# Turned gated features moved through another engine's DMA queue, and split later

## The chip, the cores and the metric

One NeuronCore of a Trainium2 chip runs the whole program. The engines are TensorE (PE, matrix products), VectorE (DVE), ScalarE (ACT), GpSimd (POOL) and SyncE (SP), each with its own queue of instructions that it works through in order. A transfer (DMA) is issued by an instruction in one of these queues; the queues of SP, ACT and POOL can issue, and an issue that waits for something holds up what stands behind it in that queue. The metric is the device time of one execution in microseconds, lower is better. Before the change it is 1006.37 us, the median of three runs (1005.99 to 1008.15).

## What is computed

A decoder trunk of two layers over 256 tokens of width 1024, in float32. Each layer is:

```
h = h + 1/2 * FFN1(norm(h))          # silu(x Wg) * (x Wu), then Wd; inner width 2816
h = h + mixer(norm(h))               # 8 stick-breaking heads and 4 latent-attention heads
h = h + 1/2 * FFN2(norm(h))
h = h + sigmoid(norm(h) Wgate) * (p[layer] Wproj)
```

A final norm follows. There are four FFNs in the program (two layers, `a` before the mixer and `b` behind it), and the change lies in them alone.

## The kernel before

**Split products.** A float32 product is made of three matmuls on reduced operands: each operand is split into a high part `h` and the rest `l`, and the sum takes high by high, high by low and low by high (`mm3`, lines 254 to 259; the three matmuls are lines 256, 257, 258). So every weight passes three engines before PE: a load by SP into a `raw` buffer (7 of them), ACT makes `wh`, DVE makes `wl`. A pair `wh`, `wl` of 1024 columns is a tile of the pool `w`, of which there are 8. `Unit.load` (from line 140) does this for plain weights (load line 148, `wh` 152, `wl` 153). `Seven` (from line 174) does it for blocks that are multiplied with seven products in place of eight; there DVE first adds and subtracts raw blocks (line 188) and then ACT and DVE split the sums (lines 193, 194; loads line 185).

**An FFN.** The inner width is cut into six blocks (`NBLK`): five of 512 columns and a last one of 256. For each block `i` PE makes the gate `g` and the up-projection `u` for both token halves `t` (0 and 1), 128 tokens each. Blocks 1 and 3 (only 3 in the first FFN of the program) are made by `wide_seven`, which starts with seven products on sums of quarters of `x` (14 calls of `mm3`) and ends with two half products (`half_mm`, 16 calls). `gated` then makes `silu(g) * u` into the tile `pr` (DVE, line 540) and calls `Gates.add`.

**Turning the features (`Gates.add`).** The down-projection needs the features on the partitions, not the tokens. `add` does it in steps: DVE transposes `pr` in blocks of 32 by 32 (line 502); a transfer `m` writes `pr` to a buffer in DRAM (line 504); four transfers read it back, one per group of 32 partitions, into the tile `a`, which the profile calls `ft` (`back`, line 509); ACT and DVE split `ft` into `fh` and `fl` (`parts`, lines 516, 517); and for blocks 1, 2, 3 the second half also makes four sums of the two halves and splits them (`sums`, lines 469 to 480). The `ft` tiles come from the tag `w2`, which has two buffers, so a block's pair must be read before the next block's pair can be written. All these transfers are issued from SP, in the same queue as the loads of the weights. A block sends 2 transfers `m` and 8 transfers `ft`; there are 24 blocks in the program.

**The down phase.** After the six blocks PE multiplies with the down weights: two chunks of block 0, then seven products on block 1, the rest of block 0, seven on block 2, block 5, seven on block 3, and block 4. Behind the first seven products everything still due is emitted (`flush`). In the middle of this phase `ple_inputs` loads `p` from SP (line 1007) into a buffer that block 0's features had.

**What sets the order.** The program is written down in PE's order. `soon(us, f)` puts a step off by so many microseconds of PE work: `mm3` adds 0.68 to a running sum for 512 columns, and steps that are due are written down there. `BACK` is the delay of `back`, `PARTS` that of `parts`, both from the call of `add`. A planner then orders each engine's queue by the order in which the program was written and by when, by its own reckoning, operands and buffers are ready. So a queue is not exactly in the written order: in the profile DVE does line 471 ahead of line 517 of the same half, for example. `after` only forbids an order; the split `fh` may not come ahead of the newest `wh` written before it.

Of the kernel before, what the change touches and what calls it, by code (L numbers as in the profile page):

```python
# [32 lines left out]

BACK, PARTS = 2.5, 7.0


def turned_order(n):
# [25 lines left out]
def trunk(ctx: ExitStack, tc: tile.TileContext, xT, xr, pT, w, gains, fgain, consts, out):  # L65
    nc = tc.nc
# [47 lines left out]
    def after(later, earlier):  # L114

        tc.add_manual_dep(later.ins, earlier.ins.name, mybir.DependencyInfo(mybir.DependencyClass.NoSync, mybir.DependencyReason.DATA), reason="order")
# [119 lines left out]
    def soon(us, f):  # L236
        due.append((pe[0] + us, len(due), f))
# [23 lines left out]
    def both(x, *ix):  # L261
        return tuple(t[ix] for t in x)
# [22 lines left out]
    def wt(tag, name, n=2, width=T):  # L285

        return tp.tile([P, 768], F32, tag=tag, name=name)[:, : n * width].rearrange("p (a b) -> p a b", a=n)
# [7 lines left out]
    def in_runs(x):  # L295

        return x.rearrange("p j (a s) -> p j a s", s=32)
# [29 lines left out]
    class Norm:  # L327
# [8 lines left out]
        def add(self, t, c):  # L336

            i = self.parts[t]
            self.parts[t] += 1
            junk = flat("w3", f"junk_{self.name}_{t}{i}", BF16)[:, : c.stop - c.start]  # L340
            return nc.scalar.activation(junk, h[:, t, c], AF.Square, accum_out=self.ss[:, t, i : i + 1])
# [90 lines left out]
    class Gates:  # L432
# [63 lines left out]
        def add(self, i, t, pr, more):  # L496


            f = self.block(i)
            n = 4 if i < NBLK - 1 else 2  # L500
            name = f"{self.tag}_{i}{t}"
            nc.vector.transpose(pr, pr)
            m = mem_p.tile([P, 4, n * 32], F32, tag="turn", name=f"m_{name}")
            nc.sync.dma_start(m, pr.rearrange("p (q r) -> p q r", q=4))
            a = wt("w2", f"ft_{name}", 4, n * 32)

            def back():
                for q in range(4):
                    nc.sync.dma_start(a[32 * q : 32 * q + 32], m[:, q].rearrange("(a f) r -> f a r", a=4))

            def parts():
                self.turned[i, t] = v = a.rearrange("p a (j s) -> p j a s", j=n)

                ks = slice(2 if i in SEVEN and t else 0, n)
                fh, fl = (in_runs(q) for q in both(f, slice(None), ks, slice(t * P, (t + 1) * P)))
                after(nc.scalar.activation(fh, v[:, ks], AF.Copy), newest_wh[0])
                nc.vector.tensor_tensor(fl, v[:, ks], fh.bitcast(F32), ALU.subtract)
                if i in SEVEN and t:
                    self.sums(i)

            soon(BACK, back)
            soon(PARTS + t, parts)

    def seven_mm(banks, x_of, ops, first, last):

# [698 lines left out]
```

## Time and profile before

| | |
|---|---|
| median of three runs | 1006.37 us |
| profiled execution, whole | 1003.63 us |
| its span, first to last instruction | 1001.8 us |
| mean granted TensorE clock | 0.996 |
| PE busy | 981.6 us (98%) |
| DVE busy | 861.9 us (86%) |
| ACT busy | 635.7 us (63%) |
| POOL busy | 12.4 us (1%), 13 instructions |
| DMA moved | 210.50 MB, 210 GB/s over the span |

The profile records one execution. A busy time is the sum of an engine's instructions; instructions that issue transfers are not counted in it. A row of the timeline gives start, duration, engine, source line, operation, output and input names, and in brackets the idle time before it with what ended it; rows with `x3` at the end hold three instructions in a row. `SPq` is SP issuing transfers. A row of the waits gives who waited for whom: total time, number of times, the longest. Line numbers are those of the kernel before.

### The profile page before, as it was taken

To read this page: it belongs to the slowest core of one execution; us is meant where nothing else is said; L and a number is where in the kernel's file an instruction comes from. 1 tells how busy PE (TensorE), PEld (TensorE's weight loads), DVE (VectorE), ACT (ScalarE), POOL (GpSimd) and SP (SyncE) were. 2 spreads that over 40 slices of the span, in tenths; PEclk is the share of its full clock that TensorE was granted. 3 is DMA by queue.
4 is the path that set the end of the run, shared out by engine and by line. 5 is a ranking of instruction groups with operands and counts; after the bars stand their busy time and mean duration, and the time that the engine had idled before them with its cause. 6 is when DMAs were issued, how large, how long until landed. Compare 5 with 4: busy or idle time off the path is not lost.

```text
span 1001.8 us, 14087 instructions
## 1 busy us (share of the span) xinstructions
PE 981.6 (98%) x4888; PEld 824.2 (82%) x4888; DVE 861.9 (86%) x1218; ACT 635.7 (63%) x974; POOL 12.4 (1%) x13
## 2 busy tenths in 40 slices
PE   9998999999999999999999999999999999999996
PEld 7875888899888888887788888888998888888875
DVE  6689999967679999799998998899676799989995
ACT  6746656848566566567676556567766755756664
POOL 0000000000100000000000000002000000000000
PEclk9999999999999999999999999999999999999999
DMA  8876875675233778685737686676733357776651
GB/s 302 302 252 202 302 231 188 230 257 175 98 127 108 268 224 274 197 259 194 262 105 264 229 272 213 212 249 210 274 106 106 126 174 251 267 240 204 222 187 43
DMA packets 88055, 210.50 MB, mean 210 GB/s; under 512 B 14000, under 2 KB 35632, under 8 KB 87984
## 3 DMA queue, kind: packets, MB, share of 16 engines
q1 hardware_dynamic: 87552, 209.03, 62.1%
q8 instruction: 38, 0.62, 0.2%
q10 hardware_dynamic: 432, 0.57, 0.2%
q14 instruction: 33, 0.27, 0.1%
HBM read 196.98 MB, written 12.58 MB: 209 GB/s over the span
## 4 chain that ended last, share of the span: by engine, by line
PE 86%; DVE 5%; DMA 4%; ACT 3%; issue 1%; SPq 0%; ACTq 0%; DVEq 0%
DMA raw<-in_w 4%; PE p_b L256 3%; PE g_a L256 3%; PE p_b L257 3%; PE g_a L258 3%; PE g_a L257 3%; PE g_b L257 3%; PE g_b L258 3%; PE g_b L256 3%; PE p_b L258 3%; PE d_a L257 3%; PE d_a L258 3%; PE d_a L256 3%; PE p_a L257 3%; PE p_a L258 3%; PE p_a L256 2%
## 5 line engine op out<-in xcount | busy, mean ns | idle before, releaser
L153 DVE TENSOR_TENSOR wl<-raw,wh 128x1024 fp32r<-128x1024 f32 (+1 forms) x278 | 321.0, 1187 | 49.5 <-ACT wh L152 48.1
L152 ACT ACTIVATE wh<-raw 128x1024 fp32r<-128x1024 f32 (+1 forms) x278 | 278.5, 1031 | 103.2 <-DMA raw<-in_w 47.4
L193 ACT ACTIVATE wh<-raw 128x1024 fp32r<-128x1024 f32 x133 | 139.0, 1058 | 130.0 <-DVE raw L188 98.9
L194 DVE TENSOR_TENSOR wl<-raw,wh 128x1024 fp32r<-128x1024 f32 x133 | 159.4, 1216 | 11.1 <-ACT wh L193 10.4
L188 DVE TENSOR_TENSOR raw<-raw,raw 128x1024 f32<-128x1024 f32 x76 | 92.6, 1220 | 4.5 <-DMA raw<-in_w 2.4
L256 PE MATMUL d_a<-wh,fh_a 128*128 128x512 f32 x108 | 42.3, 391 | 0.0
L258 PE MATMUL d_b<-wh,fl_b 128*128 128x512 f32 x108 | 42.2, 391 | 0.0
L256 PE MATMUL d_b<-wh,fh_b 128*128 128x512 f32 x108 | 42.2, 391 | 0.0
L258 PE MATMUL d_a<-wh,fl_a 128*128 128x512 f32 x108 | 42.1, 390 | 0.0
L257 PE MATMUL d_b<-wl,fh_b 128*128 128x512 f32 x108 | 42.1, 389 | 0.0
L257 PE MATMUL d_a<-wl,fh_a 128*128 128x512 f32 x108 | 42.0, 389 | 0.0
L256 PE MATMUL g_a<-wh,x0h 128*128 128x512 f32 x80 | 31.1, 390 | 0.3 <-ACT x0h L305 0.3
L257 PE MATMUL g_a<-wl,x0h 128*128 128x512 f32 x80 | 31.0, 389 | 0.0
L258 PE MATMUL g_a<-wh,x0l 128*128 128x512 f32 x80 | 31.0, 389 | 0.0
L257 PE MATMUL u_a<-wl,x0h 128*128 128x512 f32 x64 | 25.2, 394 | 0.5 <-DVE wl L153 0.5
L256 PE MATMUL g_b<-wh,x_mix0h 128*128 128x512 f32 x64 | 25.1, 392 | 0.0
L256 PE MATMUL g_b<-wh,x_mix1h 128*128 128x512 f32 x64 | 25.1, 392 | 0.0
L256 PE MATMUL g_a<-wh,xe0h 128*128 128x512 f32 x64 | 25.0, 391 | 0.0
L258 PE MATMUL u_a<-wh,x0l 128*128 128x512 f32 x64 | 25.0, 390 | 0.0
L258 PE MATMUL g_a<-wh,xe0l 128*128 128x512 f32 x64 | 24.9, 390 | 0.0
L257 PE MATMUL g_a<-wl,xe0h 128*128 128x512 f32 x64 | 24.9, 389 | 0.0
L258 PE MATMUL g_b<-wh,x_mix0l 128*128 128x512 f32 x64 | 24.9, 389 | 0.0
(552 smaller groups left out, 2683.9 us busy)
## 6 DMA issues: line engine op xcount, KB each, us to landing
raw<-in_w SPq DMA_DIRECT2D x338, 512.0 KB, 5.1
m_a<-pr_a SPq DMA_DIRECT2D x20, 256.0 KB, 2.1
ft_a<-m_a SPq DMA_DIRECT2D x80, 64.0 KB, 2.7
m_b<-pr_b SPq DMA_DIRECT2D x20, 256.0 KB, 2.3
ft_b<-m_b SPq DMA_DIRECT2D x80, 64.0 KB, 2.9
raw<-in_w SPq DMA_DIRECT2D x16, 256.0 KB, 4.4
xin<-in_xT SPq DMA_DIRECT2D x4, 256.0 KB, 4.7
h<-in_xr SPq DMA_DIRECT2D x2, 512.0 KB, 8.0
```

The costliest lines, as they stand in the source:

```text
L152: nc.scalar.activation(wh[:, a], r[:, a], AF.Copy),
L153: nc.vector.tensor_tensor(wl[:, a], r[:, a], wh[:, a].bitcast(F32), ALU.subtract),
L188: nc.vector.tensor_tensor(self.raw[o], self.raw[a], self.raw[b], op)
L193: newest_wh[0] = nc.scalar.activation(wh, r, AF.Copy)
L194: nc.vector.tensor_tensor(wl, r, wh.bitcast(F32), ALU.subtract)
L256: nc.tensor.matmul(o, ah, bh, start=start, stop=False, **kw)
L257: nc.tensor.matmul(o, ah, bl, start=False, stop=False, **kw)
L258: newest_mm[0] = nc.tensor.matmul(o, al, bh, start=False, stop=stop, **kw)
```

## The change

Two things change, in `Gates.add` and its two constants. The transfer `m` and the four transfers of `back` are issued from POOL's queue instead of SP's. `PARTS` goes from 7 to 12, and the second half's `parts` comes 3.5 after the first half's instead of 1; `BACK` stays.

```diff
-BACK, PARTS = 2.5, 7.0
+BACK, PARTS = 2.5, 12.0
...
             m = mem_p.tile([P, 4, n * 32], F32, tag="turn", name=f"m_{name}")
-            nc.sync.dma_start(m, pr.rearrange("p (q r) -> p q r", q=4))
+            nc.gpsimd.dma_start(m, pr.rearrange("p (q r) -> p q r", q=4))
             a = wt("w2", f"ft_{name}", 4, n * 32)
 
             def back():
                 for q in range(4):
-                    nc.sync.dma_start(a[32 * q : 32 * q + 32], m[:, q].rearrange("(a f) r -> f a r", a=4))
+                    nc.gpsimd.dma_start(a[32 * q : 32 * q + 32], m[:, q].rearrange("(a f) r -> f a r", a=4))
...
             soon(BACK, back)
-            soon(PARTS + t, parts)
+            soon(PARTS + 3.5 * t, parts)
```

## The prediction

> **What bounds the kernel now.** I read the page's totals first, then who TensorE (PE) waits for, then stretches of time.
>
> ```profile
> span 1001.8 us, 14087 instructions
> PE 981.6 (98%) x4888; PEld 824.2 (82%) x4888; DVE 861.9 (86%) x1218; ACT 635.7 (63%) x974; POOL 12.4 (1%) x13
> ```
> ```profile
> PE p_a L257 <- DVE wl L194: 3.8, 3, 2.0
> PE e L257 <- DVE wl L153: 1.7, 1, 1.7
> PE p_a L256 <- ACT wh L193: 1.6, 2, 1.1
> PE pv L257 <- DVE wl L153: 1.4, 2, 0.8
> ```
> PE is idle for 1001.8 - 981.6 = 20.2 us in all, so a change that feeds it better has little to win, and only where it waits: 5.4 us on `p_a`, the seven-product block of the first FFN, and 1.7 + 0.8 us on `e` and `pv` in layer 0's embedding stage. The stretches (PE, PEld, DVE, ACT, POOL busy; clock; DMA share; GB/s):
>
> ```profile
> 72.30:91.75 19.45, 13.82 (x47) 8.84 (x45) 19.27 (x26) 12.31 (x16) 0.00 (x0) 0.91 0.54 182
> 340.00:380.00 40.00, 40.00 (x178) 32.89 (x177) 38.27 (x50) 22.43 (x29) 0.00 (x0) 1.00 0.74 241
> 476.00:480.30 4.30, 2.45 (x12) 1.75 (x13) 3.84 (x16) 3.09 (x11) 0.00 (x0) 1.00 0.36 122
> ```
> ```profile
> 92.11 0.40 PE L258 MATMUL p_a<-wh,x0l 128*128 128x512 f32 x1
> 95.76 0.39 PE L257 MATMUL p_a<-wl,x0h 128*128 128x512 f32 x1
> ```
> From 92.11 to 95.76 PE makes 16 steps, 0.228 us each. In 72.30 to 91.75 it does 47 matmuls in 19.45 us; at its pace they take 10.7, so 8.7 us are lost there (idle time, slow restarts and a granted clock of 0.91). DVE is full in that stretch (19.27 of 19.45). In a block such as 340 to 380 DVE is nearly full too and PE loses nothing.
>
> Why is DVE late at 72? Three engines shortly before it:
>
> ```profile
> 43.77 1.32 SPq L148 DMA_DIRECT2D raw<-in_w  x3
> 51.94 1.14 SPq L504 DMA_DIRECT2D m_a<-pr_a  x2
> 53.19 0.38 SPq L148 DMA_DIRECT2D raw<-in_w  x1
> 54.02 5.59 SPq L509 DMA_DIRECT2D ft_a<-m_a  x8
> 59.66 0.91 SPq L148 DMA_DIRECT2D raw<-in_w  x2
> 60.61 1.89 SPq L185 DMA_DIRECT2D raw<-in_w  x4
> ```
> ```profile
> 49.98 1.06 ACT L152 ACTIVATE wh<-raw 128x1024 fp32r<-128x1024 f32 x1 [0.26 <-PE u_a L258]
> 59.40 1.06 ACT L152 ACTIVATE wh<-raw 128x1024 fp32r<-128x1024 f32 x1 [8.35 <-DMA raw<-in_w]
> ```
> ```profile
> 49.26 1.43 DVE L540 SCALAR_TENSOR_TENSOR pr_a<-u_a,hr_in,s_a 128x512 f32<-128x512 f32 x2 [2.97 <-PE u_a L258]
> 60.49 1.23 DVE L153 TENSOR_TENSOR wl<-raw,wh 128x1024 fp32r<-128x1024 f32 x1 [4.60 <-ACT wh L152]
> ```
> SP stands from 45.09 to 51.94 in front of the m transfer, which needs `pr`; it then sends one load, eight ft transfers, and six loads back to back in 2.84 us, so their buffers had long been free. ACT waits 8.35 us for a load and DVE 4.60 us for ACT. This is the wait that the change can take away.
>
> **The change, part by part.**
>
> *Loads no longer stand behind m and ft.* SP loses 48 m and 192 ft issues (24 blocks of two halves):
>
> ```profile
> L504 SPq DMA_DIRECT2D m_a<-pr_a x24: 326/327/382, 37.5 to 628.4; - x24
> L509 SPq DMA_DIRECT2D ft_a<-m_a x96: 302/424/1723, 39.5 to 634.5; - x96
> SPq L504 <- DVE pr_a L502: 63.9, 21, 10.2
> ```
> That is 48 x 0.327 + 192 x 0.424 = 97 us of issue time, and the `pr` waits besides. Nearly all of it hides under PE's stock of eight split tiles (12 matmuls, 2.73 us each), so it is worth nothing where PE never waits. In the first FFN it is worth this: at 49.98 ACT waited for PE, so all eight were full; by 59.40 PE had freed (59.40 - 49.98) / 2.73 = 3 more. With loads there, three `wl` splits of 1.15 us pitch go into DVE's idle 4.60 us: 3.45 us gained (bounds 0, if other waits keep DVE idle, and 4.60).
>
> *Splits stand later.* PARTS moves the first half's from 7 to 12 us of PE work after the block, the second half's, with the sums, from 8 to 15.5. In the lossy stretch block 2's lie ahead of DVE's last seven-product split:
>
> ```profile
> 86.48 1.02 DVE L517 TENSOR_TENSOR fl_a<-ft_a,fh_a 128x512 fp32r<-128x512 f32 x2
> 87.42 0.42 DVE L469 TENSOR_TENSOR sum_a<-ft_a 128x256 f32<-128x256 f32 x1
> 87.76 0.41 DVE L471 TENSOR_TENSOR sum_a<-ft_a,ft_a 128x256 f32<-128x256 f32 x1
> 88.09 0.42 DVE L470 TENSOR_TENSOR sum_a<-sum_a,ft_a 128x256 f32<-128x256 f32 x1
> 88.43 1.22 DVE L194 TENSOR_TENSOR wl<-raw,wh 128x1024 fp32r<-128x1024 f32 x1
> ```
> The seven products are 14 x 0.68 = 9.5 us of PE work, so at 12 and 15.5 these fall behind them: 88.43 - 86.48 = 1.95 us gained. They land among the half products, where one tile lasts PE 2.73 us and costs DVE 1.15: hidden. Without that cover they cost their 1.95 back. No later use is in danger: the last block's splits are flushed 14.96 us into the down phase and used at 29.9.
>
> *POOL issues 240 transfers.* No row shows its price d. Near rows, landing first:
>
> ```profile
> m_a<-pr_a SPq DMA_DIRECT2D x20, 256.0 KB, 2.1
> ft_a<-m_a SPq DMA_DIRECT2D x80, 64.0 KB, 2.7
> ```
> ```profile
> 201.31 0.73 POOL L814 TENSOR_TENSOR rk<-r_a,c_sb 128x256 f32<-128x256 f32 x1 [200.38 <-ACT r_a L362]
> 262.16 1.30 POOL L892 TENSOR_TENSOR qr<-r,r 128x512 f32<-128x512 f32 x1 [3.50 <-DVE r L890]
> 690.17 5.70 POOL L814 TENSOR_TENSOR rk<-r_a,c_sb 128x256 f32<-128x256 f32 x1 [426.72 <-ACT r_a L362]
> ```
> Below, SP's 0.33; above, POOL's own instruction held to 5.70 us (0.73 when free). I take 1.3, POOL's longest unhindered row, as the nearest to an engine that makes descriptors in a program. m0, m1 and eight ft then stand in one queue; ft waits for m to land, and behind it stand only more ft and the next block's m (POOL's arithmetic comes in the mixer, long after). For d below 2.1 the halves land 5d + 4.8 and 9d + 4.8 us after m's issue, which is 51.94 - 49.26 = 2.7 us after the block's products. Against 12 and 15.5 that is 2.0 and 3.7 us late at d = 1.3. ACT then waits, ahead of weight splits; the 8.35 us wait above cost PE 0.5 us at once, so 3.7 us inside a stock of eight tiles cost nothing: taken as 0. Where the next block follows 10.9 us after (the last one), its second ft transfer also waits for the w2 buffer until 4.6 us instead of 2.5: off the path.
>
> The 5.70 row shows POOL held up beside DVE. By the Trainium skill (SBUF — State Buffer, "Who interferes with whom") a DVE instruction with two SBUF inputs holds up a GpSimd instruction that reads SBUF, while descriptor generation, which writes, is held by DVE's two-port modes, which tensor_tensor does not have; by that rule the sum stays, without it the slow rival below comes true.
>
> *Layer 0's second FFN, 405 to 480.* The same block, but another wait takes its place:
>
> ```profile
> 413.65 0.84 SPq L148 DMA_DIRECT2D raw<-in_w  x2
> 419.81 0.81 SPq L504 DMA_DIRECT2D m_b<-pr_b  x2
> 421.60 3.92 SPq L509 DMA_DIRECT2D ft_b<-m_b  x8
> 425.57 1.38 SPq L185 DMA_DIRECT2D raw<-in_w  x3
> 427.04 0.97 SPq L148 DMA_DIRECT2D raw<-in_w  x2
> 436.40 0.33 SPq L1007 DMA_DIRECT2D p<-in_pT  x1
> ```
> The loads of 425.57 come some 4 us earlier, but the p transfer still holds SP until PE is done with a buffer at 436.40, and the lead ends there. Of the 2.5 us of stalls I take 0.5 (bounds 0 and 2.5).
>
> *Unknown:* what a first POOL transfer costs around the span (0 to 1.83, all that lies there; 0 taken), and orders that the planner changes elsewhere (plus or minus 2.5, the size of the second stall; 0 taken).
>
> **Sum:** 3.45 + 1.95 + 0.5 = 5.9 us. The profiled execution took 1003.63 (span 1001.8), so 997.7; the median of the runs is 2.74 above it, so 1006.37 - 5.9 = **1000.5 us**.
>
> **Rivals.**
> - *Nothing moves.* DVE is the bound at 60 to 92 and block 1's splits and sums, now later, go ahead of the seven products' and eat the lead. For it: DVE full. Against: they lay behind 60.49 before as well. 1006.4. The Trainium skill (DMA: Bandwidth & Descriptors, "Issuing engines are not separate DMA queues") speaks for it: issuing from several engines saves only the issue time. The row of 51.94 shows that here a wait is saved as well.
> - *Only the splits' place counts,* the planner leaving the loads where they were: -1.95, 1004.4.
> - *Both stalls go:* -8.7 - 2.5 = -11.2, 995.2.
> - *POOL is too slow.* The second half is 9d - 8.0 us late; above d = 1.8 that exceeds the 8.35 us which the stock covered. At d = 2.0 it is 10.0, 1.65 beyond; in the 11 stages of seven products (7 wide, 4 down), where DVE has no slack, that is +18 and the gain is gone: 1024. For it: the 5.70 row, DVE 86% busy. Against: 1.30 when free.
> - *The planner's new order opens a stall* like the one at `e`, and the first is kept: +2.5, 1009.
>
> **How the numbers follow.** Forecast 0.47 (its own range 998.5 to 1002.5), nothing 0.10, splits only 0.12, both stalls 0.10, slow POOL 0.14, new stall 0.07. No change can be told from below 0.2%, 2.0 us; the splits-only case lies on that bound and is halved. Faster 0.63, within 0.16, slower 0.21. The range 995 to 1010 leaves out slow POOL and part of the full cure.
>
> **What would show it.** Right: loads on SP between 45 and 52, no ACT wait of 8 us and no DVE wait of 4.6 us before 60, the 47 matmuls in about 14 us, POOL issues near 1.3 us. Wrong: ACT waiting many us for ft in block after block with PE idle behind it (slow POOL); the p_a waits as large as before with DVE full (nothing moves).

## The result, and the profile after

The changed kernel takes **1055.4 us** (median of 4 runs, 1051.7 to 1059.8) against 1006.2: ratio 1.0486, 95% interval 1.0440 to 1.0532. It is 49 us slower; the forecast was 1000.5, and the range ended at 1010.

The page's totals after the change:

```profile
span 1051.9 us, 14119 instructions
PE 996.9 (95%) x4888; PEld 827.2 (79%) x4888; DVE 861.5 (82%) x1218; ACT 632.0 (60%) x974; POOL 139.2 (13%) x253
```

The span grew by 50.1 us. PE does the same 4888 matmuls; its idle time rose from 20.2 to 1051.9 - 996.9 = 55.0 us, and 15.3 us more are counted as busy, 13.9 of them in matmuls that start within 5 us of a stop. ACT and DVE do the same work as before. So PE is fed late. Who waits for whom (total us, times, longest):

```profile
ACT fh_b L516 <- DMA ft_b<-m_b: 54.8, 14, 9.8
ACT fh_a L516 <- DMA ft_a<-m_a: 51.8, 15, 10.6
...
DVE fl_b L517 <- ACT fh_b L516: 39.0, 12, 7.3
DVE fl_a L517 <- ACT fh_a L516: 36.5, 10, 8.1
...
PE p_b L257 <- DVE wl L194: 8.8, 11, 2.5
PE p_a L257 <- DVE wl L194: 6.1, 7, 1.9
PE xt_b L371 <- DVE h L397: 5.3, 4, 2.2
PE p_b L256 <- DVE ch_b L587: 5.0, 2, 2.5
PE p_a L256 <- ACT xsh_a L562: 4.8, 1, 4.8
```

Before, the two ACT rows were 3.1 and 3.2 us. Now ACT stands 106.6 us in front of `ft`, DVE stands 75.5 us behind ACT, and PE mostly names `wl`: it waits for split weights, not for the features themselves. POOL is not slow. Its issues (duration min/median/max in ns), and the time from issue to landing in the page's list of transfers (KB each, us to landing):

```profile
L509 POOL DMA_DIRECT2D ft_a<-m_a x96: 548/551/574, 42.7 to 665.0; - x96
L504 POOL DMA_DIRECT2D m_a<-pr_a x24: 557/561/700, 39.4 to 657.7; - x24
```
```profile
m_a<-pr_a POOLq DMA_DIRECT2D x20, 256.0 KB, 2.8
ft_a<-m_a POOLq DMA_DIRECT2D x80, 64.0 KB, 5.7
```

An issue costs 0.55 us, but an `ft` transfer now takes 5.7 us to land, where it took 2.7 from SP.

**The first FFN**, where the prediction expected its gain: SP, POOL, ACT, DVE and PE in the same timeline.

```profile
44.24 1.46 SPq L148 DMA_DIRECT2D raw<-in_w  x2
46.51 8.87 SPq L185 DMA_DIRECT2D raw<-in_w  x4
...
43.80 3.25 POOL L509 DMA_DIRECT2D ft_a<-m_a  x6
...
52.17 0.63 ACT L516 ACTIVATE fh_a<-ft_a 128x512 fp32r<-128x512 f32 x1 [5.82 <-DMA ft_a<-m_a]
...
52.84 0.69 DVE L517 TENSOR_TENSOR fl_a<-ft_a,fh_a 128x512 fp32r<-128x512 f32 x1 [4.09 <-ACT fh_a L516]
...
79.52 0.79 PE L256 MATMUL p_a<-wh,xsh_a 128*128 128x512 f32 x1 [4.82 <-ACT xsh_a L562]
```

The loads do move ahead: SP, which stood from 45.09 to 51.94 in front of `m`, now sends five loads between 44.24 and 48.78, and stands only then, in front of a `raw` buffer (the row of 8.87 us holds that wait, 49.11 to 55.05). But ACT's 8.35 us wait for a load has become one of 5.82 us for `ft`, and DVE's 4.60 one of 4.09.

**A down phase**, where the loss is. The `ft` of block 5, both halves, are issued from 147.91 on (a row of eight issues); ahead of them a wait of block 3:

```profile
119.32 0.63 ACT L516 ACTIVATE fh_a<-ft_a 128x512 fp32r<-128x512 f32 x1 [6.42 <-DMA ft_a<-m_a]
...
147.91 4.40 POOL L509 DMA_DIRECT2D ft_a<-m_a  x8 [4.18 <-DMA m_a<-pr_a]
...
153.56 0.42 ACT L516 ACTIVATE fh_a<-ft_a 128x256 fp32r<-128x256 f32 x1 [5.61 <-DMA ft_a<-m_a]
153.88 2.94 ACT L193 ACTIVATE wh<-raw 128x1024 fp32r<-128x1024 f32 x3
...
154.01 0.42 DVE L517 TENSOR_TENSOR fl_a<-ft_a,fh_a 128x256 fp32r<-128x256 f32 x1 [2.77 <-ACT fh_a L516]
154.35 3.49 DVE L194 TENSOR_TENSOR wl<-raw,wh 128x1024 fp32r<-128x1024 f32 x3
...
155.63 0.50 PE L257 MATMUL p_a<-wl,fh_a 128*128 128x512 f32 x1 [1.11 <-DVE wl L194]
```

ACT waits 5.61 us for a split of 0.42; the three `wh` behind it are done back to back in 2.94 us as soon as it moves, so their operands had been ready. DVE loses 2.77 us, then does three `wl` in a row, and PE waits for the first. The 6.42 us wait at 119, in the plain blocks, cost PE nothing on the spot. It took from the stock. Counting the weight splits `wl` that DVE has begun when PE starts its matmul of a given number:

```
matmul of mm3 number      400    500    600
before                     49     60     70
changed                    47     57     66
changed with PARTS 36      51     59     69
```

The changed kernel is two splits short when the down phase begins (60 begun against 62, matmul 523) and four short at 600, of a pool of eight tiles. From 140 to 200 in the trace before, DVE is busy for 56.68 of 60 us, so there it cannot catch up. (The third row is an experiment below.)

To place the loss I compared the start of each matmul with that of the same number in the trace before. The lag (us), and where it grows:

```
stage                                    added
first FFN (up to 100, end of the wide 7)  -0.8   (lag +2.8 at 80, -0.8 at 100)
4 down phases (140-200, 429-480, 625-690, 905-960)   7.4 + 6.2 + 11.2 + 11.6 = 36.4
wide sevens of the later FFNs (360-380, 565-580, 850-890)  5.5 + 2.8 + 5.4 = 13.7
everything else                          -0.2
at 960 us of the trace before            +49.1
```

Nothing is lost in plain blocks. All of it is lost in the stages with seven products and at the end of the down phases, where PE waits 9.5 us in all for `h` (`xt_a` and `xt_b`; no such wait before).

### The profile page after: what moved, and what is told of

Same layout as the page of the kernel before. It is cut to its first block, busy times and chain, and to the rows that moved or that the text cites. A ratio compares the mean times of both kernels' runs of the same rounds, so it can differ in the third digit from the quotient of the medians.

```text
span 1051.9 us, 14119 instructions
## 1 busy us (share of the span) xinstructions
PE 996.9 (95%) x4888; PEld 827.2 (79%) x4888; DVE 861.5 (82%) x1218; ACT 632.0 (60%) x974; POOL 139.2 (13%) x253
## 4 chain that ended last, share of the span: by engine, by line
PE 37%; issue 24%; DVE 17%; DMA 15%; ACT 4%; POOL 2%; SPq 0%; POOLq 0%; ACTq 0%; DVEq 0%
DVE wl L194 5%; DMA raw<-in_w 4%; DMA ft_b<-m_b 4%; DVE wl L153 4%; DVE raw L188 3%; DMA ft_a<-m_a 3%; ACT wh L152 2%; DMA m_b<-pr_b 2%; PE e L258 1%; PE e L256 1%; PE e L257 1%; DMA m_a<-pr_a 1%; PE g_a L258 1%; PE g_a L256 1%; PE g_b L257 1%
## 5 line engine op out<-in xcount | busy, mean ns | idle before, releaser
L152 ACT ACTIVATE wh<-raw 128x1024 fp32r<-128x1024 f32 (+1 forms) x278 | 278.8, 1030 | 101.5 <-DMA raw<-in_w 35.3
L193 ACT ACTIVATE wh<-raw 128x1024 fp32r<-128x1024 f32 x133 | 136.8, 1053 | 115.5 <-DVE raw L188 112.1
L509 POOL DMA_DIRECT2D ft_a<-m_a x96 | 52.4, 553 | 29.9 <-DMA m_a<-pr_a 21.2
L509 POOL DMA_DIRECT2D ft_b<-m_b x96 | 52.4, 553 | 29.3 <-DMA m_b<-pr_b 17.0
L504 POOL DMA_DIRECT2D m_a<-pr_a x24 | 13.6, 566 | 275.2 <-DVE pr_a L502 274.4
L504 POOL DMA_DIRECT2D m_b<-pr_b x24 | 13.5, 563 | 258.2 <-DVE pr_b L502 257.5
L516 ACT ACTIVATE fh_b<-ft_b 128x512 fp32r<-128x512 f32 (+1 forms) x24 | 12.9, 536 | 54.8 <-DMA ft_b<-m_b 54.8
L517 DVE TENSOR_TENSOR fl_b<-ft_b,fh_b 128x512 fp32r<-128x512 f32 (+1 forms) x24 | 13.9, 578 | 39.0 <-ACT fh_b L516 39.0
L516 ACT ACTIVATE fh_a<-ft_a 128x512 fp32r<-128x512 f32 (+1 forms) x24 | 12.9, 537 | 51.8 <-DMA ft_a<-m_a 51.8
L517 DVE TENSOR_TENSOR fl_a<-ft_a,fh_a 128x512 fp32r<-128x512 f32 (+1 forms) x24 | 13.8, 576 | 36.5 <-ACT fh_a L516 36.5
```

The source lines that it names most:

```text
L152: nc.scalar.activation(wh[:, a], r[:, a], AF.Copy),
L193: newest_wh[0] = nc.scalar.activation(wh, r, AF.Copy)
L504: nc.gpsimd.dma_start(m, pr.rearrange("p (q r) -> p q r", q=4))
L509: nc.gpsimd.dma_start(a[32 * q : 32 * q + 32], m[:, q].rearrange("(a f) r -> f a r", a=4))
```

## The experiments

The ratios are to the kernel before, run on the same chip, with 95% intervals.

### Which part does it: the queue or the later splits

Queue alone:

```diff
-            nc.sync.dma_start(m, ...)        +            nc.gpsimd.dma_start(m, ...)
-                    nc.sync.dma_start(a[...  +                    nc.gpsimd.dma_start(a[...
 BACK, PARTS = 2.5, 7.0      # and PARTS + t, as before
```

> Only the queue is changed: m and ft from POOL, splits where they were (7 and 8 us). Theory A (ScalarE parks at the split fh until the turned features land, which through POOL's queue is some 13 us after m against 8 on SyncE, with weight splits behind it): the earlier splits meet the same late landing, so ScalarE waits for ft as long as in the changed kernel (106 us) or longer, and the time is 1050 or more. Theory B (the later splits themselves do the harm, by falling into stages where VectorE has no slack): the waits on PE go and the time is 1000 to 1010.

Measured 1057.1, ratio 1.0511 (1.0490 to 1.0532); ACT waits 104.9 us for `ft`. In ACT's queue each `fh` stands behind the same number of weight splits as in the changed kernel, or one more or less, although PARTS is 7 here.

Later splits alone, all transfers on SP:

```diff
-BACK, PARTS = 2.5, 7.0
+BACK, PARTS = 2.5, 12.0
-            soon(PARTS + t, parts)
+            soon(PARTS + 3.5 * t, parts)
```

> Only the splits are moved: 12 and 15.5 us, all transfers on SyncE as before. Theory A: ft lands 8 us after m, long before 12, ScalarE waits for ft under 10 us in all, and the time is within 5 us of before (1001 to 1011). Theory B: most of the loss is here, 1035 to 1055, with TensorE waiting for wl in the seven-product stages of the down phases.

Measured 1008.3, ratio 1.0016 (1.0006 to 1.0026). The first FFN gains 1.5 us (1.95 forecast), and 1.4 at 180 to 200, 2.2 at 440 to 480 and 0.8 at 560 to 580 are lost. So the queue costs the 49 us, and the later splits are worth about nothing at this size.

### Which of the transfers

Only `m` on POOL (`ft` on SP, PARTS 7 and t), then only `ft` on POOL (`m` on SP), then only `m` on POOL with the read-back and the splits somewhat later (BACK 4.5, PARTS 8.5, t):

> Half of the queue change, splits at 7 and 8 us: m goes from POOL, the four ft stay on SyncE. SyncE no longer stands in front of m for pr, and ft keeps its place in line among the loads. Theory A: ft lands 2.7 us after its issue as before, the stall of the first FFN at 72 to 92 us shrinks by 3 to 6 us, and the time is 1000 to 1004. If POOL's queue itself is what costs (a late m): ft is late by the 0.7 us that m lands later, SyncE waits in front of ft instead of in front of m, and the time is 1006 to 1015.

> The other half of the queue change alone, splits at 7 and 8 us: m stays on SyncE, the four ft go from POOL. Sharing theory: it is ft's place that costs. ft takes 5 us or more where loads run beside it, ScalarE waits for it more than 60 us, and the time is 1030 to 1055. If moving m is what costs, it is 1000 to 1010.

> The kernel with m on POOL and ft on SyncE, but ft written 2 us later (BACK 4.5) and the splits 1.5 later (8.5 and 9.5), so that loads may go ahead of an ft that still waits for m; SyncE stood 106 us in front of ft with BACK at 2.5. If that wait costs anything: below 998.4, 993 to 997. If it is hidden under the stock of split tiles: 997 to 1000, no change. If ft now lands too late for its split: 1002 or more, with ScalarE waiting for ft.

Measured: `m` alone **998.4**, ratio 0.9924 (0.9908 to 0.9941), below the 1000 to 1004 expected; `ft` alone 1056.0, 1.0496 (1.0469 to 1.0522), just above its 1030 to 1055; `m` with BACK 4.5 997.8, 0.9917 (0.9902 to 0.9932), not to be told from `m` alone. The whole loss is in `ft`'s queue; `m`'s move is a gain that the change threw away. The transfers of the kernel with only `m` moved, and its first FFN:

```profile
ft_a<-m_a SPq DMA_DIRECT2D x80, 64.0 KB, 2.0
```
```profile
43.92 1.38 SPq L509 DMA_DIRECT2D ft_a<-m_a  x3
45.40 2.27 SPq L148 DMA_DIRECT2D raw<-in_w  x5
57.98 3.65 SPq L509 DMA_DIRECT2D ft_a<-m_a  x8
...
75.90 0.50 PE L257 MATMUL p_a<-wl,xsh_a 128*128 128x512 f32 x1 [2.18 <-DVE wl L194]
```

This is the test of the prediction's main term. SP sends five loads at 45.40, in the stretch in which it stood before, and ACT's 8.35 us wait is gone (waits of at most 1.79 us are left). DVE does use the early loads: at matmul 240 it has begun 32 weight splits against 29 before. But then it waits, in its own order, for a feature split that in ACT's queue stands behind work on PE's results:

```profile
62.02 0.69 DVE L517 TENSOR_TENSOR fl_a<-ft_a,fh_a 128x512 fp32r<-128x512 f32 x1 [2.70 <-ACT fh_a L516]
```

Before, DVE began the same instruction at 61.63, and at matmul 280 both have begun 33. PE's waits on `p_a` for split weights are 4.7 us against 5.6, and at 100 us this kernel is 0.2 us behind the one before. **With the splits early, the freed loads are worth nothing there.** The gain of this kernel is elsewhere: 3.1 us at 460 to 480 (the stalls at `e` and `pv`), 1.7 at 680 to 700, 1.3 at 940 to 980.

### Does that gain come from the load of p

In the trace before SP waits 18.5 us in all in front of the two loads of `p` (line 1007), with `m` on POOL 0.6. So `p` alone on POOL, `m` and `ft` on SP:

```diff
-        nc.sync.dma_start(pr, pT[L])
+        nc.gpsimd.dma_start(pr, pT[L])
```

> The kernel before with one edit: the load of p (line 1007, two of them in the run) is issued from GpSimd. In the trace before, SP stands 8.3 us in front of the first one (428.1 to 436.4) with the weight loads behind it. Theory (the 3.1 us that the kernel with only m on GpSimd gains at 460 to 480 come from SP no longer standing in front of p): 3 us here at the same place and as much at the second layer's end, 1000 to 1003 us, with m and ft on SP as before. Rival (that gain comes from m's waits leaving SP): within 1 us of the kernel before, 1005 to 1007.

Measured 1009.3, ratio 1.0030 (1.0015 to 1.0045): 3.0 us slower, which neither expectation had, and both stalls are there:

```profile
479.69 0.50 PE L257 MATMUL pv<-wl,xpsbk 128*128 128x512 f32 x1 [1.33 <-DVE wl L153]
483.46 0.51 PE L257 MATMUL e<-wl,x_b0h 128*128 128x512 f32 x1 [1.67 <-DVE wl L153]
```

The theory falls: taking that wait out of SP's queue does not bring the gain. The same 3.07 us at 460 to 480 also appear in four kernels further down that leave `p` on SP (half loads on SP, late order on SP, and the last two); what removes the stalls there is not settled.

### Why ft lands late

First rival: POOL's way of making transfers is slow. So `m` and `ft` from ACT's queue, the rest as in the changed kernel:

```diff
-            nc.gpsimd.dma_start(m, ...)      +            nc.scalar.dma_start(m, ...)
-                    nc.gpsimd.dma_start(a... +                    nc.scalar.dma_start(a...
```

> As the changed kernel, but m and ft are issued from ScalarE's hardware queue, so they have a queue of their own without POOL's program making the descriptors. If the late landing comes from sharing the DMA engines with weight loads in another queue, ft takes 5 to 7 us to land here too. If it comes from the software path, 2.5 to 3.5 us as on SyncE. The time is not decided by this alone, since ScalarE now waits for pr and m in its own queue: 1010 to 1060.

Measured 1082.8, ratio 1.0760 (1.0736 to 1.0785). The time, above the 1010 to 1060 expected, says little itself, since ACT now also issues 240 transfers between its splits. The landing was expected at 5 to 7 us or at 2.5 to 3.5:

```profile
ft_a<-m_a ACTq DMA_DIRECT2D x80, 64.0 KB, 4.6
ft_b<-m_b ACTq DMA_DIRECT2D x80, 64.0 KB, 4.5
```

That lies between the two ranges and decides nothing. So I sorted the `ft` transfers of each trace by the number of weight loads in flight (issued and not yet landed) when the `ft` was issued (median landing in us, count in brackets; the second row is an experiment below, `m` on POOL with PARTS 36):

```
loads in flight               none         one          two        three or more
before, ft on SP            1.93 (37)   2.95 (151)   3.87 (4)        -
ft on SP, PARTS 36          1.94 (109)  2.87 (41)    4.53 (32)   5.08 (10)
changed, ft on POOL         2.19 (27)   3.46 (27)    5.04 (57)   7.22 (81)
ft on ACT                   1.96 (35)   3.57 (81)    5.65 (54)   6.54 (22)
```

Without a load in flight, `ft` lands in about 2 us from any queue; POOL's way costs 0.2. With loads in flight it lands late from every queue, and POOL is no slower than ACT up to two of them. So POOL's way is not the cause. Two things are. One is the moment of the issue: SP, which stood in front of `m` and `ft`, sent 188 of its 192 `ft` transfers with at most one load in flight; POOL sends 138 of 192 with two or more. The other is the queue: with as many loads in flight, `ft` takes some 0.5 to 2 us longer from a queue beside the loads' own. The traces show part of how. With one load in flight, a further load that SP issues within 2 us of the `ft` goes with a later landing from POOL (4.18 us against 2.79 without one) and from ACT (4.71 against 3.51), but not from SP (2.31 against 3.31). What I infer: in SP's queue that load stands behind the `ft`, from another queue it shares the DMA engines with it. How much each is worth can be estimated: SP's medians (the two and three columns from the second row), weighed by POOL's counts, give 4.2 us; POOL's own give 5.3, SP's before 2.8. So some 1.4 of the 2.5 us are the moment and 1.1 the queue.

If the loads are the cause, fewer bytes must shrink the loss. So the loads of plain weight tiles at half their bytes, in the changed kernel and, as control, in the kernel before; the second half of each such tile is left out of the computation, the first is split twice in its place:

```diff
-            newest_load[0] = nc.sync.dma_start(r, w[self.u, :, a : a + n])
+            newest_load[0] = nc.sync.dma_start(r[:, : n // 2], w[self.u, :, a : a + n // 2])
...
+                r2 = r[:, : n // 2].unsqueeze(1).to_broadcast([P, 2, n // 2])
```

> As the changed kernel, but each plain weight load moves half its bytes and ScalarE and VectorE read that half twice, so their work and PE's is the same; the second half of each such tile of weights is left out of the computation. Sharing theory (ft through another queue is slow because the weight loads take the DMA engines beside it): ft lands in 3 to 4.5 us in the median in place of 5.5, ScalarE waits for ft under 60 us, and the time falls to 1010 to 1035. If POOL's own path is slow: ft still takes 5.5 us, the waits stay near 100 us and the time at 1045 or more.

> The kernel before (all of it on SP) with the loads of the plain weight tiles cut to half their bytes: each half that is loaded is read twice by the splits, and the second half of these tiles is left out of the computation. It is the control for the changed kernel with half loads, 1012.9 us. Theory (a transfer in a second queue shares the engines with the loads, so the loss grows with the loads beside it): this kernel gains little from half loads, some 990 to 1000 us, and the changed kernel with half loads then stands 13 to 23 us above it, against 49 with whole loads. Rival (half the loads make every version faster by the same 40 us, and the loss does not hang on the loads): some 964 us, and the distance stays near 49.

Measured: changed with half loads 1012.9, ratio 1.0077 (1.0058 to 1.0097); before with half loads 986.5, 0.9806 (0.9791 to 0.9821). Their distance is 26.3 us, against 49 with whole loads. So the loss hangs on the loads, about half of it on half the plain bytes (the seven-product loads stayed whole); the 13 to 23 us of the expectation were too low, because the kernel before gained more from half loads (986.5) than the 990 to 1000 expected. The landing and ACT's waits in the changed one (its lines behind 153 count one higher):

```profile
ft_a<-m_a POOLq DMA_DIRECT2D x80, 64.0 KB, 3.6
...
ACT fh_a L517 <- DMA ft_a<-m_a: 36.8, 14, 5.7
ACT fh_b L517 <- DMA ft_b<-m_b: 27.6, 14, 5.1
```

3.6 us in place of 5.7, and 64.4 us of waits in place of 106.6, where under 60 was expected.

### Who pays: the place of the splits in ACT's queue

The changed kernel with PARTS 16 in place of 12:

> As the changed kernel (m and ft from POOL), with the splits later still: 16 and 19.5 us in place of 12 and 15.5. ft lands 10.6 and 13.0 us after m in the mean, at most 16.9, and m goes some 2.7 us after the block's products. Theory A (ScalarE parks at fh until ft lands): fh now stands behind more weight splits, the waits of ScalarE for ft fall from 106 us to under 50, and the time falls to 1010 to 1035. If where the split is written does not decide its place in ScalarE's queue (the planner puts it where it reckons that ft has landed): the waits stay near 100 us and the time stays at 1050 or more.

Measured 1055.0, ratio 1.0488 (1.0469 to 1.0506), and ACT still waits 99.0 us for `ft`. ACT's order of instructions is the same as with PARTS 12, each `fh` behind the same number of weight splits: the planner puts the split where by its reckoning `ft` is there, and 7, 12 or 16 does not bind. That was no test of a later place. With 36 and with 44, the rule that `fh` may not precede the newest `wh` written before it does bind; the `fh` of blocks 0 to 3 then stand behind 3 to 8 weight splits more with 36 and behind 5 to 12 more with 44, those of blocks 4 and 5 behind 0 to 5 more:

```diff
-BACK, PARTS = 2.5, 12.0
+BACK, PARTS = 2.5, 36.0        # second run: 44.0
```

> The changed kernel with PARTS 36 in place of 12: the splits fh then stand behind 3 to 5 more weight splits in ACT's queue in the down products (PARTS 16 had left ACT's order as it was). Nothing else is different: queues and loads are those of the changed kernel. Theory (PE pays because ACT, in order, stands in front of the late ft with weight splits behind it): ACT's waits for ft fall from 106 us to below 30, and the time to 1005 to 1025 us. Rival (the late ft itself, or the sharing of the engines with the loads, is what PE pays): ACT's waits fall as well, but the time stays at 1045 to 1056.

> As the last one with PARTS 44, 7 or more weight splits later than in the changed kernel. Theory: ACT's waits for ft are next to nothing, and if the splits are not yet so late that the products wait for them the time is the same as or a little below that with PARTS 36, 1000 to 1020 us; if they are, PE's waits name fh or fl and the time goes up again. Rival (sharing of the engines is itself the price): 1045 to 1056.

Measured **1010.5** (ratio 1.0040, 1.0025 to 1.0055) and 1010.2 (1.0037, 1.0020 to 1.0053). With 36:

```profile
ACT fh_a L516 <- DMA ft_a<-m_a: 13.8, 5, 5.3
ACT fh_b L516 <- DMA ft_b<-m_b: 13.0, 4, 6.6
...
ft_a<-m_a POOLq DMA_DIRECT2D x80, 64.0 KB, 5.5
ft_b<-m_b POOLq DMA_DIRECT2D x80, 64.0 KB, 4.6
```

`ft` still lands late (the halves 10.2 and 13.7 us after `m`'s issue in the mean, 10.6 and 13.0 in the changed kernel) and the queues are those of the changed kernel, but ACT's waits fall from 106.6 to 26.8 us, DVE's waits for `fh` behind them from 75.5 to 1.1, and 45 of the 49 us come back. So PE pays because ACT, in order, stands in front of a late `ft` with ready weight splits behind it. (The next section takes from these 45 us what the late place is worth without a late `ft`: 8.7.) The last block's wait in the first down phase is still there, at 141.65, and not much shorter:

```profile
141.65 0.42 ACT L516 ACTIVATE fh_a<-ft_a 128x256 fp32r<-128x256 f32 x1 [4.32 <-DMA ft_a<-m_a]
...
139.64 2.35 DVE L194 TENSOR_TENSOR wl<-raw,wh 128x1024 fp32r<-128x1024 f32 x2
142.10 0.42 DVE L517 TENSOR_TENSOR fl_a<-ft_a,fh_a 128x256 fp32r<-128x256 f32 x1
```

But here ACT was far enough ahead: DVE still had splits to do while ACT waited and reached `fl` without a wait of its own, where it lost 2.77 us in the changed kernel. PE loses 1.5 us by 200 where it had lost 7.4. So a wait of ACT that DVE does not feel cost nothing here. At 44 nothing more is gained: ACT's waits are 32.2 us there, not next to nothing as expected.

### The order alone, and what the parts are worth together

What does the late order do where `ft` is not late? All on SP with PARTS 36 and 3.5 t; then with only `m` on POOL:

> The kernel before, all on SP, with the late order of the splits alone (PARTS 36, 3.5 t). Theory (ft on SP lands early, so that ACT hardly waited and the order takes nothing away that PE paid; later splits only leave less room before the products): 1000 to 1008 us, ACT's waits for ft near 0, a gain in the first FFN of 2 to 5 us that is partly lost in the later down products. Then the queue itself, at this order, costs the rest up to 1010.5: some 2 to 10 us. Rival (late splits are worth as much on SP as on GpSimd, and the order was what was wrong in both): 990 us or below, a gain as large as the 45 us' share that a shorter wait in front of m would give.

> m on GpSimd, ft on SP, PARTS 36 and 3.5 t everywhere. Theory: the first FFN gains most of the 8 us that the changed kernel with PARTS 36 showed there if that gain is the order's, and the later down products lose 1 to 3 us each as there: 992 to 1000 us. Rival (the gain in the first FFN comes from ft leaving SP): the first FFN gains under 2 us, and the time is 998 to 1005.

Measured 997.7 (ratio 0.9911, 0.9896 to 0.9925) and 994.3 (0.9874, 0.9858 to 0.9891). In medians:

```
                       splits early (7, t)   splits late (36, 3.5 t)
all on SP                   1006.4                  997.7
m on POOL                    998.4                  994.3
m and ft on POOL            1057.1                 1010.5
```

With all on SP the time is below the 1000 to 1008 expected and above the rival's 990. Read down: with `m` on POOL, moving `ft` as well costs 58.7 us at the early place and 16.2 at the late one. Read across: the late place brings 46.6 us with `ft` on POOL, and 8.7 even on SP, where ACT's waits for `ft` had been 6.3 us only; so some 38 of the 46.6 hang on the late `ft`. The first FFN of the kernel with all on SP and late splits (timeline of SP and ACT, then the stretch 72.30 to 91.75: PE, PEld, DVE, ACT, POOL busy; clock; DMA share; GB/s):

```profile
46.36 0.86 SPq L148 DMA_DIRECT2D raw<-in_w  x2
51.83 1.15 SPq L504 DMA_DIRECT2D m_a<-pr_a  x2
...
51.73 1.06 ACT L152 ACTIVATE wh<-raw 128x1024 fp32r<-128x1024 f32 x1 [4.88 <-DMA raw<-in_w]
...
72.30:91.75 19.45, 17.85 (x78) 14.24 (x77) 19.14 (x26) 14.41 (x19) 0.00 (x0) 1.00 0.68 223
```

SP still stands in front of `m` (46.36 + 0.86 to 51.83) and ACT still waits 4.88 us for a load, but PE does 78 matmuls in the stretch in which it did 47, and has gained 7.3 us by 100. So most of the stall that the prediction read there was made by DVE's order, with block splits and sums ahead of seven-product splits. The freed loads come in second: from 60 to 100 PE gains 0.3 us with `m` on POOL alone, 7.8 with the late order alone and 10.0 with both. Nearly all of the late order's gain is lost again at 140 to 200, where the kernel with all on SP falls back by 6.8 us; what it keeps comes later, the largest part 3.07 us at 460 to 480.

So the late order in the first FFN only, `m` on POOL, the rest early; first with `ft` of that FFN on POOL, then with all `ft` on SP:

```diff
-            nc.sync.dma_start(m, ...)        +            nc.gpsimd.dma_start(m, ...)
-            soon(PARTS + t, parts)
+            soon(36.0 + 3.5 * t if self.tag == "a0" else PARTS + t, parts)
```

> m on GpSimd everywhere; in the first FFN ft on GpSimd too, with PARTS 36 and 3.5 t; in the others ft on SP with PARTS 7 and t. If the parts add up: 998 (m alone on GpSimd) less the 8 us of the first FFN, 989 to 992. Rival (the two gains are the same one, or the first FFN's is given back at its end): 996 to 1000.

> As the last one with ft of the first FFN on SP as well: only the order there is late. If the order brings the 8 us: as the last one, 989 to 992 us. If ft has to leave SP for it: 996 to 999, as m alone.

Measured 991.2 (ratio 0.9849, 0.9834 to 0.9863) and **991.0** (0.9847, 0.9833 to 0.9862). The gains add up, and the queue of the first FFN's `ft` makes no difference. The last one beats both kernels, with the change's own two ideas in other places:

```profile
span 988.8 us, 14110 instructions
PE 976.8 (99%) x4888; PEld 824.7 (83%) x4888; DVE 862.5 (87%) x1218; ACT 635.5 (64%) x974; POOL 38.9 (4%) x61
```

PE is idle for 12.0 us in it, against 20.2 before. Open remains what else `ft`'s own queue costs at the late place (the 16.2 us): PE names `xt <- DVE h` for 8.2 us there, and DVE waits 25.0 us for loads of raw blocks (0.8 and 8.9 us with only `m` on POOL), but no run takes these apart.

## Why the prediction was wrong, point by point

**The step that failed** is "3.7 us inside a stock of eight tiles cost nothing: taken as 0". The landing itself was not underrated. With its d = 1.3 the prediction had the halves landing 5d + 4.8 = 11.3 and 9d + 4.8 = 16.5 us after `m`'s issue; they landed 10.6 and 13.0 us after it on average (6.7 and 8.0 before). That came of two errors that cancel: an issue costs 0.55 us and not 1.3, and `ft` lands in 5.7 and not in SP's 2.7; that the sum came near was luck. ACT then waited 3.7 us on average, where 2.0 and 3.7 were forecast, but 29 times and up to 10.6 us. What a wait of ACT ahead of the weight splits costs was then judged by one row, the 8.35 us wait at 51 that cost PE 0.5 at once, in a stretch of plain blocks. In plain blocks it held: nothing is lost there. But ACT's waits hold up DVE as well, 75.5 us in all, and the weight splits fall behind: two short at the first down phase, four short inside it. In the seven-product stages DVE is full and cannot make that up, and those stages, with the end of the down phases, take all of the 49 us. PARTS 36 alone, at nearly the same landing, shortened ACT's waits to 26.8 us and brought back 45; the late place is worth 8.7 of them with all on SP.

**The landing in another queue** was priced by a row of the same queue, where SP's own standing had kept loads away from `ft`. The trace before has one transfer of another queue beside loads, 47 KB of `g_sb` from ACT at the start, which landed in 3.2 us; the prediction did not use it, and gave bounds to d, but none to the landing. The Trainium skill (DMA: Bandwidth & Descriptors, "Issuing engines are not separate DMA queues") says that transfers of different issuing engines run on the same 16 engines and interleave, and that a second issuer saves only issue time. The prediction took it as a reason for "nothing moves". The runs agree with the interleaving, and here it has a price: 7.2 us of landing with three or more loads in flight, 2.2 with none.

**Where a split stands.** The prediction compared the landing with 12 and 15.5 us, as if PARTS set the place. Between 7 and 16, with `ft` on POOL, it does not set it at all (by one weight split at most).

**Freed loads, 3.45 us:** 0 with the splits early, the prediction's lower bound and for the reason that it gave, other waits of DVE. With `m` on POOL three more splits were there at matmul 240 and none at 280. In the changed kernel ACT's wait for `ft` took the place of the wait for the load. Once the splits are late the same loads bring 2.2 us. That ACT's wait alone made the lossy stretch 20 us later was read from their order in time.

**Later splits, 1.95 us:** right in kind, too small. PARTS 12 brought 1.5 in the first FFN, PARTS 36 brings 7.3 there. That is most of the 8.7 us of the stall, and the granted clock of that stretch is 1.00 again. The changed kernel gained 3.6 us at 80 to 100, and had lost 2.8 by 80; the queue alone, with PARTS 7, gains 4.3 there, so that gain is not due to PARTS.

**Layer 0's second FFN, 0.5 us:** in the changed kernel nothing of it is to be seen under the 6.2 us lost there. That the load of `p` ends the lead was not confirmed: moved out of the way, the two stalls stayed as they were.

**The slow-POOL rival** (1024) had the right chain, ACT waiting for `ft` and PE idle in the seven-product stages, and the wrong cause. POOL is fast. Its 5.70 us row did not carry over: no `ft` issue took over 0.574 us beside a DVE that is 82% busy, as the Trainium skill has it (SBUF — State Buffer, "Who interferes with whom") for descriptor generation beside two-input operations. Its condition, d above 1.8, was one way to be late; the other had no rival.

## What to carry to other kernels

A transfer that others wait for has a price in its queue: before it goes to a queue of its own, ask how many loads will be in flight when it is issued there, and give its landing a bound that does not come from the old queue. When an operand comes late, do not ask how late but what stands behind the instruction that waits for it, add the waits up against the stock that hides them, and price the sum in the stage where that stock cannot be refilled, not where one wait was seen to be harmless. Read a stall from the order of the full engine just before it, and do not join it to an earlier wait without a run that removes the wait alone; what such a run shows as worthless can still be worth something behind another cure, as the freed loads were.

## What was not expected of the hardware

A transfer issue on POOL took 0.55 us, 548 to 574 ns over 96 of them, against 0.30 to 1.72 us (median 0.42) on SP for the same ones. With no load in flight when it was issued, an `ft` transfer (64 KB, 32 in the last blocks) landed in 1.9 us from SP, 2.0 from ACT and 2.2 from POOL; with two in flight in 3.9 to 4.5, 5.65 and 5.0; with three or more in 5.1 (ten transfers), 6.5 and 7.2. Halving the bytes of the plain loads took POOL's 64 KB transfers from 5.7 to 3.6 us.
